# The last projection of a hybrid decoder layer in two sweeps, with seven products in place of eight in some of its quads

## The chip, the core and the metric

One core of a Trainium2 chip runs the whole layer. The metric is device time in microseconds: the median of several executions, here 1580.53 us for the kernel before (three runs, 1578.45 to 1582.09).

## What is computed

One layer of a conditioned decoder on 256 tokens of width 2048, all in float32: a modulated RMS norm, one wide projection, a gated recurrent branch and a sliding-window attention branch, their merge, and a gated feed-forward part. The change touches the end of it:

```python
gate, up = jnp.split(h2 @ w_ffn_in[l], 2, axis=-1)        # 256 x 5632 each
x = x + g2 * ((jax.nn.silu(gate) * up) @ w_ffn_out[l])    # 5632 x 2048
...
return rms_norm(x, final_g)
```

The projection of this document is the product with `w_ffn_out`: 256 tokens (two row blocks of 128, `t`), 5632 hidden channels (44 k blocks of 128, `kt`) and 2048 columns (four column blocks of 512, `n`).

## The kernel before

**Products in parts.** TensorE multiplies in the reduced float32 format (`fp32r`). To keep precision each operand is split in a high part (a cast) and a low part (the difference), and a product is three matmuls: high x high, high x low, low x high (`mm3`, L320). The weights come from memory as raw float32 in pieces of 128 x 1024 (512 KB). ScalarE (ACT) casts the high part (`do_hi`, L271 to L280; the profile shows it as line 277) and VectorE (DVE) subtracts for the low part (`do_lo`, L282 to L293, line 289). The activations are split once, after they are made.

**Items and buffers.** Every piece of weight is an item, a tuple in the list `items`: source, columns, a function that issues its matmuls, what comes after it, whether its parts are kept, and a weight for the planner. `step(i)` (L300) writes the program for item i in this order: stages of earlier results that are due (`run_posts`, one stage of each per step), the load of item i+5, the high part of item i+3, the low part of item i+2, fetches of other streams, and the matmuls of item i. Each engine executes its own instructions in the order in which they were written. There are five raw buffers, four for high parts and three for low parts (L43), so these steps run ahead of the matmuls by that much and no more. A planner's clock with assumed costs (L64, L198) decides only where side work is placed that has no fixed position; in the last projection all that is placed so is the fetch of the residual and of the final gain.

**The gate and up projections.** 11 pairs of slabs (L1110). After each pair `up_f_post` (L1096) multiplies, transposes on TensorE, and `parts_of` (L870) makes high and low parts of 4 k blocks, `fh` and `fl`, the stationary operands of the last projection. These 22 tiles stay in a pool of 25 equal buffers (`b4`).

**The last projection.** A first sweep over all 44 k blocks makes three column blocks (n = 0, 1, 2) for both row blocks, in six PSUM banks (`pf`): per two k blocks two items from `w_f2a` (columns 0 to 1023) and one from `w_f2b` (two k blocks of columns 1024 to 1535). `first_blocks` (L1178) then adds these blocks to the residual `x2`, squares them for the norm on ACT and multiplies with the final gain, while a second sweep makes the last column block from `w_f2c` (`pl`). There the last eight k blocks (`EARLY` = 36 on) are computed for row block 0 only; their weights are kept. `early_rows` (L1219) adds what row block 1 has by then. Its last eight k blocks come at the very end, in two halves of 256 columns (`late`, L1224), while row block 0 is finished (`finish_first`, L1205). `finish_last` (L1234) ends row block 1. An add is a pair of DVE instructions: multiply with the gate `bcs[5]` (tile `pa`), then add to `x2` (L1167, L1169).

```python
for k, (l, w) in enumerate(((ah, hi), (ah, lo), (al, hi))):
    for _, n, c0 in mine:
        ...
        nc.tensor.matmul(
            fin[t, n], lhsT=l[:, rows(t)], rhs=w[:, c0:c0 + 512], start=kt == 0 and k == 0,
```

Of the kernel before, what the change touches and what calls it, by code (L numbers as in the profile page):

```python
# [9 lines left out]
F32 = mybir.dt.float32  # L10
# [56 lines left out]
@with_exitstack  # L67
def hybrid_layer(
    ctx: ExitStack, tc, vecs, x_t, x_r, ada_k, ada_t, ada_g, w_in, bv_row, bm_row, bg_row, lru_w, w_lru, w_att, w_o,
    w_f1, w_f2a, w_f2b, w_f2c, fg_row, out,  # L70
):
    nc = tc.nc
    ctx.enter_context(tc.manual_schedule())
# [33 lines left out]
    def rows(t):  # L107
        return slice(t * P, (t + 1) * P)
# [149 lines left out]
                    break  # L258


    items = []
    live = {}
    at = {"load": 0, "hi": 0, "lo": 0}

    def do_load(i):
        src, cols = items[i][0], items[i][1]
        raw = wp.tile([P, CH], F32, tag="raw", name=f"raw{i}", bufs=AHEAD - 1)
        nc.sync.dma_start(raw[:, :cols], src)
        live[i] = [raw, None, None, load_time(cols)]

    def do_hi(i):  # L271
        cols, keep = items[i][1], items[i][4]
# [4 lines left out]
        nc.scalar.copy(hi[:, :cols], live[i][0][:, :cols])  # L277
        clock["act"] = max(clock["act"], live[i][3])
        charge(0, cols * T_ACT)
        live[i][1], live[i][3] = hi, clock["act"]  # L280

    def do_lo(i):  # L282
        cols, keep = items[i][1], items[i][4]
# [5 lines left out]
        nc.vector.tensor_tensor(lo[:, :cols], raw[:, :cols], f32(hi[:, :cols]), op=ALU.subtract)  # L289
# [3 lines left out]
        live[i][0] = None  # L293

    def upto(what, fn, n):
        while at[what] < min(n, len(items)):
# [1 line left out]
            at[what] += 1  # L298

    def step(i):  # L300
        _, cols, mm, post, _, weight = items[i]
# [8 lines left out]
        end = clock["pe"] + cols * T_PE * weight  # L310
        mm(hi, lo)
        run_sides(end)
        clock["pe"] = end
        if post is not None:
            posts.append(post())

    def in_rows_of(bank):
        return bank.rearrange("p j n -> p (j n)")
# [7 lines left out]
    def add_slab(slab, name, act, k0, k1, post, in_rows=False, before=None, late=0):  # L326

        banks = []

        def products(a, b):  # L330
            def go(hi, lo):
                if a == k0 + late and before is not None:
                    before()
                if a == k0:
                    banks.extend(wtile(f"{name}_{k0}_{i}") for i in range(2))
                parts = [(kt, f) for kt in range(a, b) for f in range(2 if in_rows else 4)]
                if b == k1:
# [12 lines left out]
            return go  # L350

        for a in range(k0, k1, 2):
            b = min(a + 2, k1)
            items.append((
                slab[:, a * 512:b * 512], (b - a) * 512, products(a, b), (lambda: post(banks)) if b == k1 else None,
                False, 1,
            ))


# [719 lines left out]
        posts.append(rest())  # L1079


    f_hi, f_lo, silu = {}, {}, {}


    def h2act(kt):
# [10 lines left out]
    def up_f_post(s):  # L1096
        def post(banks):
            sg = silu.pop(s)
            for t in range(2):
                nc.vector.tensor_tensor(sg[:, t, :], in_rows_of(banks[t]), sg[:, t, :], op=ALU.mult)  # L1100
            yield 1.4, 0
            yield 0, 0
            pts = turned(sg, f"ft{s}_")
            yield 0, 0
            fh, fl = b4(f"fh{s}", F32R), b4(f"fl{s}", F32R)
            yield from parts_of(pts, fh, fl)
            f_hi[s], f_lo[s] = fh, fl
        return post

    for s in range(11):  # L1110
# [7 lines left out]
    def last_first():  # L1118
        ada_ffn.finish(streams[-1].fetch)
        last = hp.tile([P, 4, D], F32, tag="h", name="last")  # L1120
        fin["x2"], fin["fg"] = last[:, 0:2, :], last[:, 2, :]
        fin["ss"] = const.tile([P, 2, 5], F32, name="ss3")
        for n in range(3):
            for t in range(2):
                pool, tag = ((ps_w, "w"), (ps_m, "m"))[n // 2]
                fin[t, n] = pool.tile([P, 512], F32, tag=tag, name=f"pf{t}{n}")

    def fetch_last():
        yield 0, 0
# [2 lines left out]
            yield 0, 0  # L1132
            nc.sync.dma_start(fin["x2"][:, t, :], x1d[rows(t), :])


    N_HOLD = 4
    EARLY = NH - 2 * N_HOLD

    def out_products(jobs, t2=(0, 1), hold=None, after=None):

        def go(hi, lo):
            if hold is not None:
                hold.extend((hi, lo, j) for j in jobs)
            if jobs[0][0] == 0 and jobs[0][1] == 0:
                last_first()
                sides.append(Side(fetch_last()))
            for t in t2:
                for kt in sorted({j[0] for j in jobs}):
                    ah, al = fact(kt)
                    mine = [j for j in jobs if j[0] == kt]  # L1150
                    for k, (l, w) in enumerate(((ah, hi), (ah, lo), (al, hi))):
                        for _, n, c0 in mine:
                            if (t, n) not in fin:
                                fin[t, n] = mtile(f"pl{t}")
                            nc.tensor.matmul(  # L1155
                                fin[t, n], lhsT=l[:, rows(t)], rhs=w[:, c0:c0 + 512], start=kt == 0 and k == 0,
                                stop=kt == (EARLY if (t, n) == (1, 3) else NH) - 1 and k == 2,
                            )
            if after is not None:
                after()  # L1160
        return go

    def add_block(t, ps, c0, cols, dst=None):

# [10 lines left out]
        yield  # L1175
        nc.scalar.activation(y, x2, AF.Square, accum_out=fin["ss"][:, t, n:n + 1])

    def first_blocks():  # L1178
        for n in range(3):
            for t in range(2):  # L1180
                g = residual(t, n)
                next(g)
                yield 1.2, 0
                next(g, None)
                yield 0, 0.7
        for t in range(2):
            x2 = fin["x2"][:, t, :3 * 512]
            nc.vector.tensor_tensor(x2, x2, fin["fg"][:, :3 * 512], op=ALU.mult)
            yield 1.7, 0

    for kt in range(0, NH, 2):
        for i in range(2):
            items.append((w_f2a[kt + i], CH, out_products([(kt + i, 0, 0), (kt + i, 1, 512)]), None, False, 1))
        items.append((
            w_f2b[kt // 2], CH, out_products([(kt, 2, 0), (kt + 1, 2, 512)]),
            first_blocks if kt == NH - 2 else None, False, 1,
        ))
    held = []

# [58 lines left out]
            elif i < 2:  # L1258
                nc.scalar.dma_start(out[rows(1), cs], x2[:, cs])

    for kt in range(0, NH, 2):
        late = kt >= EARLY
        items.append((
            w_f2c[kt // 2], CH,
            out_products(
                [(kt, 3, 0), (kt + 1, 3, 512)], (0,) if late else (0, 1), held if late else None,
                last_rows if kt == NH - 2 else None,
            ),
            early_rows if kt == EARLY - 2 else None, late, 0.5 if late else 1,
        ))  # L1270


# [95 lines left out]
    sides.extend((hmod, ada, ada_ffn))  # L1368
    for i in range(len(items)):
        step(i)  # L1370
    finish_first()
    finish_last()


def _layout(i):
# [8 lines left out]
        return w.reshape(NK, P, n, 512).transpose(2, 1, 0, 3).reshape(n, P, NK * 512)  # L1384

    def pairs(w):
        return w.reshape(NH // 2, 2, P, 512).transpose(0, 2, 1, 3).reshape(NH // 2, P, CH)

    ada_w, ada_b = f("ada_w")[0], f("ada_b")[0]
    vecs = np.concatenate(  # L1390
# [17 lines left out]
        "w_f2b": pairs(w2[:, CH:CH + 512]), "w_f2c": pairs(w2[:, CH + 512:]),  # L1408
        "fg_row": f("final_g"),
    }  # L1410
    return {k: np.ascontiguousarray(v) for k, v in made.items()}
# [19 lines left out]
```

## Time and profile before

| | |
|---|---|
| median of three runs | 1580.53 us |
| the profiled execution | 1578.05 us |
| its span, first to last instruction | 1576.3 us |
| granted TensorE clock, mean | 0.998 |
| memory traffic | 394.73 MB read, 4.20 MB written |

The profile comes from one execution. Its page gives busy times of the engines (PE is TensorE's matmul, PEld its weight load, DVE VectorE, ACT ScalarE, SP the queue that issues loads) and the chain that ended last. Groups of instructions are listed as line, engine, operation, output and inputs, with count, busy time, mean duration of one, and the idle time before them with what ended it. Matmuls overlap, so their durations add up to more than the time they take.

### The profile page before, as it was taken

The numbers are of one execution on the slowest core, as the hardware profiler recorded it, in microseconds if no ns is written. First come the engines' busy times: TensorE is split into PE (matmuls) and PEld (weight loads), VectorE is DVE, ScalarE is ACT, GpSimd is POOL, SyncE is SP. The second block draws the span as 40 slices with busy tenths as digits, with TensorE's granted clock in tenths as the row PEclk, the third lists the DMA queues.
The fourth block names the chain that finished last, engine by engine and source line by source line (L and its number), as shares of the span: only waits on it lengthen the run. The fifth ranks groups of instructions, "written<-read, shape, count | busy, mean of one in ns | idle before, by whom it ended". The sixth has DMA issues, their size and how long they took to land.

```text
span 1576.3 us, 21711 instructions
## 1 busy us (share of the span) xinstructions
PE 1559.2 (99%) x8151; PEld 1338.9 (85%) x8151; DVE 1123.1 (71%) x1427; ACT 760.2 (48%) x960; POOL 3.8 (0%) x9
## 2 busy tenths in 40 slices
PE   8999999999999999999999999999999999999997
PEld 7999999998877878888888887888888888888886
DVE  7889989899888888998558985454544555444465
ACT  4654444767855455443456444444444444333343
POOL 0000000000000000000000000000000000000000
PEclk9999999999999999999999999999999999999999
DMA  9999987665877898998768996666666666655553
GB/s 366 352 325 333 341 305 267 233 238 166 291 270 254 291 321 295 355 343 292 277 214 274 336 343 208 190 187 195 190 187 188 188 190 248 215 199 189 198 187 121
DMA packets 112908, 400.37 MB, mean 254 GB/s; under 512 B 12433, under 2 KB 12577, under 8 KB 112417
## 3 DMA queue, kind: packets, MB, share of 16 engines
q1 hardware_dynamic: 112514, 398.46, 74.0%
q8 instruction: 64, 1.05, 0.3%
q10 hardware_dynamic: 288, 0.52, 0.1%
q14 instruction: 42, 0.34, 0.1%
HBM read 394.73 MB, written 4.20 MB: 253 GB/s over the span
## 4 chain that ended last, share of the span: by engine, by line
PE 95%; DMA 3%; DVE 1%; ACT 0%; issue 0%; SPq 0%; DVEq 0%; ACTq 0%
PE pf L1155 11%; PE wi L324 6%; PE wi L323 6%; PE wi L322 6%; PE fu L322 5%; PE fu L323 5%; PE fu L324 5%; PE fg L324 5%; PE fg L322 5%; PE fg L323 5%; PE pl L1155 3%; PE wga L324 2%; PE wga L323 2%; PE wga L322 2%; PE wo L322 2%; PE wo L323 2%
## 5 line engine op out<-in xcount | busy, mean ns | idle before, releaser
L289 DVE TENSOR_TENSOR lo<-raw,hi 128x1024 fp32r<-128x1024 f32 (+1 forms) x540 | 650.1, 1207 | 390.3 <-PE pf L1155 95.6
L277 ACT CAST hi<-raw 128x1024 fp32r<-128x1024 f32 (+1 forms) x540 | 560.8, 1040 | 744.1 <-PE fu L324 141.8
L322 PE MATMUL wi<-h_both,hi 128*128 128x256 f32 x800 | 227.4, 284 | 1.7 <-ACT acc L498 1.7
L324 PE MATMUL wi<-h_both,lo 128*128 128x256 f32 x800 | 226.7, 283 | 2.0 <-DVE lo L289 2.0
L323 PE MATMUL wi<-h_both,hi 128*128 128x256 f32 x800 | 226.4, 283 | 0.0
L324 PEld LDWEIGHTS wi<-h_both,lo 128*128 128x128 f32 x800 | 153.5, 192 | 2.4 <-DVE lo L289 2.4
L322 PEld LDWEIGHTS wi<-h_both,hi 128*128 128x128 f32 x800 | 153.5, 192 | 2.1 <-ACT acc L498 1.9
L323 PEld LDWEIGHTS wi<-h_both,hi 128*128 128x128 f32 x800 | 153.5, 192 | 0.2
L322 PE MATMUL fg<-hi,h_both 128*128 128x512 f32 x352 | 138.4, 393 | 0.1
L322 PE MATMUL fu<-hi,h_both 128*128 128x512 f32 x352 | 137.8, 391 | 0.0
L324 PE MATMUL fg<-hi,h_both 128*128 128x512 f32 x352 | 137.1, 389 | 0.0
L323 PE MATMUL fg<-lo,h_both 128*128 128x512 f32 x352 | 137.0, 389 | 0.0
L324 PE MATMUL fu<-hi,h_both 128*128 128x512 f32 x352 | 137.0, 389 | 0.0
L323 PE MATMUL fu<-lo,h_both 128*128 128x512 f32 x352 | 136.9, 389 | 0.0
L409 DVE CUSTOM_DVE_ANT_0 aw<-aw,crow,modc 128x1024 f32<-128x1024 f32 x79 | 100.9, 1280 | 5.2 <-DMA aw<-in_ada_t_dram 5.2
L409 DVE CUSTOM_DVE_ANT_0 aw<-aw,crow,vec 128x1024 f32<-128x1024 f32 x79 | 100.6, 1278 | 3.6 <-DMA aw<-in_ada_t_dram 3.6
L1155 PE MATMUL pf<-hi,fh 128*128 128x512 f32 x264 | 88.5, 389 | 0.0
L1155 PE MATMUL pf<-hi,fl 128*128 128x512 f32 x264 | 88.4, 389 | 0.0
L1155 PE MATMUL pf<-lo,fh 128*128 128x512 f32 x264 | 88.4, 389 | 0.0
L322 PEld LDWEIGHTS fu<-hi,h_both 128*128 128x128 f32 x352 | 66.1, 188 | 14.1 <-issue 0.5
L323 PEld LDWEIGHTS fu<-lo,h_both 128*128 128x128 f32 x352 | 66.1, 188 | 14.1 <-issue 0.5
L324 PEld LDWEIGHTS fg<-hi,h_both 128*128 128x128 f32 x352 | 66.1, 188 | 14.0 <-DVE h_both L1054 0.2
(243 smaller groups left out, 2418.9 us busy)
## 6 DMA issues: line engine op xcount, KB each, us to landing
raw<-in_w_f_dram SPq DMA_DIRECT2D x176, 512.0 KB, 3.5
raw<-in_w_in_dram SPq DMA_DIRECT2D x164, 512.0 KB, 6.8
aw<-in_ada_t_dram SPq DMA_DIRECT2D x158, 512.0 KB, 6.3
raw<-in_w_f2a_dram SPq DMA_DIRECT2D x44, 512.0 KB, 3.2
raw<-in_w_lru_dram SPq DMA_DIRECT2D x32, 512.0 KB, 6.6
raw<-in_w_att_dram SPq DMA_DIRECT2D x32, 512.0 KB, 8.4
raw<-in_w_o_dram SPq DMA_DIRECT2D x32, 512.0 KB, 4.4
aw<-in_ada_g_dram SPq DMA_DIRECT2D x32, 512.0 KB, 6.6
```

The lines of the kernel that those rows point to most:

```text
L277: nc.scalar.copy(hi[:, :cols], live[i][0][:, :cols])
L289: nc.vector.tensor_tensor(lo[:, :cols], raw[:, :cols], f32(hi[:, :cols]), op=ALU.subtract)
L322: nc.tensor.matmul(ps, lhsT=lh, rhs=rh, start=start, stop=False, skip_group_check=True)
L323: nc.tensor.matmul(ps, lhsT=lh, rhs=rl, start=False, stop=False, skip_group_check=True)
L324: nc.tensor.matmul(ps, lhsT=ll, rhs=rh, start=False, stop=stop, skip_group_check=True)
L409: nc.vector.tensor_tensor_reduce(out=r, in0=r, in1=crow[:, j * CH:(j + 1) * CH], op0=ALU.mult, op1=ALU.add, scale=1.0, scalar=dst if j els ...
L1155: nc.tensor.matmul(fin[t, n], lhsT=l[:, rows(t)], rhs=w[:, c0:c0 + 512], start=kt == 0 and k == 0, stop=kt == (EARLY if (t, n) == (1, 3) e ...
```

## The change

The last projection goes in two sweeps of 1024 columns, n = 0 and 1 from `w_f2a`, then n = 2 and 3 from a new array `w_f2d` (the first 36 k blocks of columns 1024 to 2047). The last eight k blocks of n = 2 and n = 3 stay as they were, four items from `w_f2b` and four from `w_f2c`.

A quad is two row blocks x two k blocks x two column blocks: eight products of a 128 x 128 block with a 128 x 512 block, 24 matmuls. In 8 of the 22 quads of the first sweep and 8 of the 18 in the second (k = 6, 10, ..., 34, `SEVEN`) it is done by Strassen's scheme in Winograd's form with seven products, 21 matmuls. Its quad has four items in place of two: the two raw pieces (of the first only 512 columns are used by itself) and two pieces of differences that DVE makes from them. The seven stationary operands are the blocks and their sums (`fs`, made in `up_f_post` from the transposed activations), which are split into parts again in each sweep (`parts_high` on ACT, `parts_low` on DVE), two and one or two items ahead. Four products (p, q, r, u) accumulate over all eight quads in four PSUM banks of their own, the other three go to the blocks' own banks. After the last such quad of a sweep `combined` adds them up: a copy on ACT, four sums and four add pairs on DVE, in six stages. In the second sweep `early_rows` follows as a seventh.

The item tuple becomes a class. In `step` a new stage `made` stands between load and high part and writes the differences for item i+4, and the items' `before` functions stand behind the low part. The differences lie in the unused fourth row of the tile `last`. `first_blocks` becomes `blocks(n0, n1)`: residual, squares and gain for n = 0 and 1 after the first sweep, and for n = 2 after the last full item.

```diff
+N_MADE, N_HOLD = 5, 4
+SEVEN = tuple(range(6, 36, 4))
+EARLY = NH - 2 * N_HOLD
...
+    def do_made(i):
+        src = items[i].src
+        if callable(src):
+            clock["dve"] = max(clock["dve"], live[i - 1][3])
+            live[i][0] = src(i)
...
         upto("load", do_load, i + AHEAD)
+        upto("made", do_made, i + N_MADE)
         upto("hi", do_hi, i + N_HI)
         upto("lo", do_lo, i + N_LO)
+        for stage in it.before:
+            charge(*stage())
...
+            fc, fs = b4(f"fc{s}", F32R, (2, 2, S)), b4(f"fs{s}", F32, (8, P))
+            nc.scalar.copy(fc[:, 0], pts[0])
+            nc.scalar.copy(fs[:, 0:2, :], pts[1][:, :, 0:P])
+            nc.scalar.copy(fs[:, 2, :], pts[1][:, 1, P:])
+            yield 0, 1.3
+            nc.vector.tensor_tensor(fc[:, 1], pts[0], f32(fc[:, 0]), op=ALU.subtract)
...
+            nc.vector.tensor_tensor(s1, a21, a22, op=ALU.add)
+            nc.vector.tensor_tensor(s3, a21, a11, op=ALU.subtract)
+            nc.vector.tensor_tensor(s2, s1, a11, op=ALU.subtract)
+            nc.vector.tensor_tensor(s4, a12, s2, op=ALU.subtract)
...
+        def parts_high():
+            made["hi"] = wp.tile([P, 8, P], F32R, tag="araw", name=f"ah{sweep}_{k}", bufs=N_ADA)
+            nc.scalar.copy(made["hi"][:, 0:7, :], f_sum[k][:, 0:7, :])
+            return 0, 0.9
+
+        def parts_low():
+            made["lo"] = b4(f"al{sweep}_{k}", F32R, (8, P))
+            nc.vector.tensor_tensor(
+                made["lo"][:, 0:7, :], f_sum[k][:, 0:7, :], f32(made["hi"][:, 0:7, :]), op=ALU.subtract
+            )
+            return 1.0, 0
...
+        def first(i):
+            x = fin["made"][:, 0:CH]
+            a, b = live[i - 2][0], live[i - 1][0]
+            made["a"], made["b"] = a, b
+            nc.vector.tensor_tensor(x[:, 0:512], a[:, 512:], a[:, 0:512], op=ALU.subtract)
+            nc.vector.tensor_tensor(x[:, 512:], a[:, 512:], b[:, 512:], op=ALU.subtract)
...
+        def second(i):
+            y, x, b = fin["made"][:, CH:], made["x"], made["b"]
+            nc.vector.tensor_tensor(y[:, 0:512], b[:, 512:], x[:, 0:512], op=ALU.subtract)
+            nc.vector.tensor_tensor(y[:, 512:], b[:, 0:512], y[:, 0:512], op=ALU.subtract)
+            return y
+
+        items[-3].before.append(parts_high)
+        items[-2].before.append(parts_low)
+        half = 0.5
+        items.append(Item(src[k], CH, products((0, 0, "p")), weight=half / 2, used=512))
+        items.append(Item(src[k + 1], CH, products((1, 0, "00"), (6, 512, "01")), weight=half))
+        items.append(Item(first, CH, products((3, 0, "r"), (5, 512, "u")), weight=half))
+        items.append(Item(
+            second, CH, products((4, 0, "q"), (2, 512, "10")), (lambda: combined(n)) if k == SEVEN[-1] else None, weight=half,
+        ))
...
+        yield 0, 0.6
+        add(0, 0, pq)
+        nc.vector.tensor_tensor(pq, fin["q"], pq, op=ALU.add)
+        yield 1.8, 0
+        nc.vector.tensor_tensor(pqu, fin["u"], pq, op=ALU.add)
+        nc.vector.tensor_tensor(pqr, fin["r"], pq, op=ALU.add)
+        nc.vector.tensor_tensor(pqur, fin["r"], pqu, op=ALU.add)
+        yield 1.8, 0
+        add(0, 1, pqr)
+        yield 1.2, 0
+        add(1, 0, pqu)
+        yield 1.2, 0
+        add(1, 1, pqur)
...
+    for n, src in ((0, w_f2a), (2, w_f2d)):
+        for k in range(0, NH if n == 0 else EARLY, 2):
+            if k in SEVEN:
+                seven(k, n, src)
+                continue
+            for kt in (k, k + 1):
+                items.append(Item(
+                    src[kt], CH, out_products([(kt, n, 0), (kt, n + 1, 512)]), blocks(0, 2) if kt == NH - 1 else None,
+                ))
+    for i, k in enumerate(range(EARLY, NH, 2)):
+        items.append(Item(
+            w_f2b[i], CH, out_products([(k, 2, 0), (k + 1, 2, 512)]), blocks(2, 3) if k == NH - 2 else None,
         ))
```

More of the change, by code (lines that the diff above doesn't have):

```diff
@@ L282, in do_lo @@
     def do_lo(i):
-        cols, keep = items[i][1], items[i][4]
+        cols, keep = items[i].used, items[i].keep
         if keep:
@@ L309, in step @@
         clock["pe"] = max(clock["pe"], t)
-        end = clock["pe"] + cols * T_PE * weight
-        mm(hi, lo)
+        end = clock["pe"] + it.cols * T_PE * it.weight
+        it.mm(hi, lo)
         run_sides(end)
         clock["pe"] = end
-        if post is not None:
-            posts.append(post())
+        if it.post is not None:
+            posts.append(it.post())
     def in_rows_of(bank):
@@ L1120, in last_first, with bank @@
         last = hp.tile([P, 4, D], F32, tag="h", name="last")
-        fin["x2"], fin["fg"] = last[:, 0:2, :], last[:, 2, :]
+        fin["x2"], fin["fg"], fin["made"] = last[:, 0:2, :], last[:, 2, :], last[:, 3, :]
         fin["ss"] = const.tile([P, 2, 5], F32, name="ss3")
[L1123 to L1126, printed above, removed]
+    def bank(t, n):
+        if (t, n) not in fin:
+            fin[t, n] = (ps_w if n < 2 else ps_m).tile([P, 512], F32, tag="wm"[n // 2], name=f"pf{t}{n}")
+        return fin[t, n]
     def fetch_last():
@@ new lines, in combined, with add @@
+    def combined(n):
+        v = [b4(f"v{n}{i}", F32, (2, 512)) for i in range(2)]
+        pq, pqu, pqr, pqur = v[0][:, 0, :], v[0][:, 1, :], v[1][:, 0, :], v[1][:, 1, :]
+        nc.scalar.copy(pq, fin["p"])
+        def add(t, j, x):
+            y = sp.tile([P, 512], F32, tag="t2", name=f"yv{n}{t}{j}")
+            x2 = fin["x2"][:, t, (n + j) * 512:(n + j + 1) * 512]
+            nc.vector.tensor_tensor(y, x, bcs[5][:, (n + j) * 512:(n + j + 1) * 512], op=ALU.mult)
+            nc.vector.tensor_tensor(x2, y, x2, op=ALU.add)
+        yield 0, 0.6
[11 more added lines that the diff above has]
+        add(1, 1, pqur)
+        free(b4=2)
+        yield 1.2, 0
+        if n == 2:
+            yield from early_rows()
@@ L1259, in finish_last @@
                 nc.scalar.dma_start(out[rows(1), cs], x2[:, cs])
[L1261 to L1269, printed above, removed]
+    for i, k in enumerate(range(EARLY, NH, 2)):
+        items.append(Item(
+            w_f2c[i], CH,
+            out_products([(k, 3, 0), (k + 1, 3, 512)], (0,), held, last_rows if k == NH - 2 else None), keep=True, weight=0.5,
         ))
@@ L1370, in hybrid_layer @@
         step(i)
+    run_posts()
+    assert not posts
     finish_first()
```

101 lines of the change are left out of this document (63 added, 38 removed).

## The prediction, made before the result was known

> **What bounds the kernel now.** I read the page first, for the engine that is never free.
>
> ```profile
> span 1576.3 us, 21711 instructions
> ...
> PE 1559.2 (99%) x8151; PEld 1338.9 (85%) x8151; DVE 1123.1 (71%) x1427; ACT 760.2 (48%) x960; POOL 3.8 (0%) x9
> ...
> PE 95%; DMA 3%; DVE 1%; ACT 0%; issue 0%; SPq 0%; DVEq 0%; ACTq 0%
> ```
>
> PE is busy for 99% of the span and carries 95% of the chain that ended last. The change touches the last projection, so I looked at the chain from 1300 us on.
>
> ```profile
> 1327.27 5.44 PE pf L1155 x24
> 1332.71 0.87 PE ft L867 x8
> 1333.59 174.09 PE pf L1155 x768
> 1507.68 54.42 PE pl L1155 x240
> 1562.10 0.12 PE late L322
> ...
> 1567.87 0.02 issue
> 1567.89 0.44 DVE y L1167
> ...
> 1570.82 0.40 DVE last L1255
> ```
>
> The projection is 24 + 768 + 240 = 1032 matmuls of 512 columns without a gap, then 48 of 256 columns, then a short DVE and ACT tail. The pace is 174.09 / 768 = 0.2267 us for one matmul. (The groups of the page say 389 ns for one, but neighbours overlap: the pace is what a removed matmul gives back.)
>
> Next, what the other engines do there: the windows, the waits, and the queue that loads.
>
> ```profile
> 1333.59:1507.68 174.09, 174.09 (x769) 144.14 (x769) 79.85 (x68) 67.69 (x66) 0.00 (x0) 1.00 0.59 207
> 1507.68:1562.10 54.42, 54.42 (x243) 45.00 (x242) 35.03 (x34) 24.81 (x33) 0.00 (x0) 1.00 0.43 151
> ```
>
> ```profile
> ACT hi L277 <- PE pf L1155: 107.8, 65, 1.7
> DVE lo L289 <- PE pf L1155: 95.6, 64, 2.6
> ```
>
> ```profile
> SPq L268 <- DVE lo L289: 184.8, 81, 3.4
> ```
>
> The columns after a window's length are busy time of PE, PEld, DVE and ACT. In the first window DVE works 80 of 174 us and ACT 68. Both spend the rest waiting for PE to give back a buffer (95.6 us in 64 waits, 1.49 us each), and the loads in turn wait for DVE to free a raw buffer. So everything here is paced by PE, at a granted clock of 1.00, and a matmul that is not issued is time gained as long as DVE stays ahead. That is the question, because the change pays for the matmuls with DVE work.
>
> **PE: what is removed.** A quad of blocks (two row blocks of the tokens, two k blocks, two column blocks) had 8 products of 3 matmuls, 24 x 0.2267 = 5.44 us. With seven products it has 21, 4.76 us. In 16 quads 48 matmuls go: 48 x 0.2267 = 10.88 us. The eight-product quads only change order, and the loads keep their bytes and sizes (88 of 512 KB). The new products run three matmuls in a row on one bank, as the gate and up projections do already:
>
> ```profile
> L323 PE MATMUL fg<-lo,h_both 128*128 128x512 f32 x352 | 137.0, 389 | 0.0
> ...
> L1155 PE MATMUL pf<-hi,fh 128*128 128x512 f32 x264 | 88.5, 389 | 0.0
> ```
>
> One costs 389 ns in both orders, so I take the same pace. The Trainium skill (TensorE: Matmul & The Clock Gate, "Wait — 56ns, not 53.3ns?") gives 215.7 ns for 512 columns at the full clock; the trace paces them at 226.7, and by the page's figure, as an estimate, the cut would be 10.4 us.
>
> **DVE: what is added.** Its durations overlap as well, so I went to a stretch where it works without a break.
>
> ```profile
> 406.21 1.26 DVE L839 TENSOR_TENSOR gate<-wgl,bm 128x512 f32<-128x512 f32 x2
> 407.38 2.35 DVE L289 TENSOR_TENSOR lo<-raw,hi 128x1024 fp32r<-128x1024 f32 x2
> 409.65 1.22 DVE L713 TENSOR_TENSOR uc<-uc,acc 128x1024 f32<-128x1024 f32 x1
> ```
>
> ```profile
> 1556.68 0.69 DVE L1167 TENSOR_TENSOR y<-pl,pa 128x512 f32<-128x512 f32 x1 [4.83 <-PE pl L1155]
> 1557.41 0.69 DVE L1169 TENSOR_TENSOR last<-y,last 128x512 f32<-128x512 f32 x1
> 1558.02 2.35 DVE L289 TENSOR_TENSOR lo<-raw,hi 128x1024 fp32r<-128x1024 f32 x2
> ```
>
> From start to start a 1024-column subtraction takes (409.65 - 407.38) / 2 = 1.14 us. A 512-column one takes (407.38 - 406.21) / 2 = 0.585 to 1558.02 - 1557.41 = 0.61, so 0.60. One that reads what the instruction before it wrote starts 0.73 after that (1557.41 - 1556.68), so such a dependence costs 0.13 more. An 896-column one lies between, at 1.00 us.
>
> The seven-product quads alternate with eight-product ones. One such pair has six items in place of four, and this work for DVE: five low parts of 1024 columns (5.70), one of 512 for the first item (0.60), four 512-column differences of raw weights, one dependent (4 x 0.60 + 0.13 = 2.53), and the low part of the seven sums of activations (1.00). The sum is 9.83 us. PE has 45 matmuls in the pair, 10.20 us. So DVE goes from 4 x 1.14 of 10.88 us (42%) to 96%, with 0.37 us to spare per pair, some 34 ns for each of its 11 instructions. ACT:
>
> ```profile
> L277 ACT CAST hi<-raw 128x1024 fp32r<-128x1024 f32 x85 | 89.4, 1055 | 131.0 <-PE pf L1155 107.8 <-PE pl L1155 13.3 <-issue 6.3
> ...
> L873 ACT CAST fh<-ft 128x512 fp32r<-128x512 f32 x2 | 1.1, 586 | 0.0
> ```
>
> Five high parts at 1.055, one at 0.59 and the sums' high part at under 1.06 are 6.9 us of 10.20: no bound. Loads: four per 10.20 us, issued up to five buffers ahead, so this landing time stays covered.
>
> ```profile
> raw<-in_w_f2a_dram SPq DMA_DIRECT2D x41, 512.0 KB, 3.2
> ```
>
> The differences wait for two landed loads; behind them on DVE stand low parts that are needed two items later, and the loads left at least two items earlier. I price these waits at nothing; uncovered, each would cost up to 3.2 us less the 2.7 us of two short items.
>
> Does 96% hold under the buffers? There are three low-part buffers, so the low part of item i+3 starts when item i's matmuls have used theirs. The tightest case is the third item of a quad: behind it PE has 3 + 6 matmuls, 2.04 us, and one more before a low part is read (0.23), against 1.23 us for the subtraction. I walked the queue in program order with these times: each low part is ready 0.2 to 1 us before its matmul, so PE does not stop in the steady pairs. That is my forecast for them.
>
> **Where DVE falls behind.** Two places have more than the steady work.
>
> Start of the second sweep: the first sweep's two column blocks are added to the residual there, during the first three quads. DVE must do, up to the low part of the second item of the first seven-product quad, four add pairs (4 x 1.33), two 1024-column products with the final gain (2.28), both pairs of differences (2.53), the sums' low part (1.00) and six low parts (5 x 1.14 + 0.60): 17.4 us. PE needs 72 + 3 + 1 matmuls, 17.2 us. With a hand-over of about 0.2 us at the start the stall is 0.4 us.
>
> The end: the second sweep's seven products are combined while only four full items and four half items are left. Before the low part of the last half item DVE has six low parts (6.84), four add pairs and two residual pairs (6 x 1.33 = 7.98) and four combinations (2.53): 17.35 us, starting level. PE gets there after 48 + 18 + 1 matmuls, 15.2 us. So PE waits about 2.2 us at the last half item. Then a block of 1.33 and two products of 0.60 still stand in the queue, 2.5 us, against 1.4 us of matmuls. The residual of the first row block begins 1.2 us late, and these rows show what that meets:
>
> ```profile
> 1565.80 0.48 DVE L1216 TENSOR_SCALAR last<-last,r 128x512 f32<-128x512 f32 x1
> 1566.19 0.42 DVE L1167 TENSOR_TENSOR y<-late,pa 128x256 f32<-128x256 f32 x1
> 1566.64 0.42 DVE L1169 TENSOR_TENSOR last<-y,last 128x256 f32<-128x256 f32 x1
> 1567.89 0.42 DVE L1167 TENSOR_TENSOR y<-late,pa 128x256 f32<-128x256 f32 x1 [0.82 <-PE late L324]
> ```
>
> DVE had 0.82 us of slack before the last product; 1.2 late leaves 0.4 us on the end.
>
> Everything else I cost at nothing. The first sweep's combination (four pairs and four sums, 7.9 us) runs beside four quads of eight products, where DVE has 5.44 - 2.28 = 3.2 us free in each; uncovered it would cost the excess over 12.6 us, so nothing below that. The new preparation of eight slabs of activations replaces two subtractions by one and four of 128 columns, and runs beside the gate and up projections:
>
> ```profile
> 1000.00:1150.00 150.00, 150.00 (x676) 124.47 (x675) 74.62 (x68) 63.51 (x67) 0.00 (x0) 1.00 0.62 190
> ```
>
> DVE is half idle there. Even at 0.69 us for each of the four, a slab takes 2.1 us more; uncovered, the eight would cost 17 us, which a window with half of DVE free and PE busy throughout excludes.
>
> **The sum.** -10.88 + 0.4 + 2.2 + 0.4 = -7.9 us. The profiled execution took 1578.05 us (its span 1576.3 and 1.75 around it), so it would become 1570.2. It lies 2.5 us under the median of the runs, 1580.53; for the median I predict **1572.6 us**. A measurement of this kernel can tell about 0.2%, 3.2 us, from no change.
>
> **The rivals.**
>
> *DVE becomes the bound.* If instructions on DVE ran one after the other with their whole durations, a pair would need the sum of these:
>
> ```profile
> L289 DVE TENSOR_TENSOR lo<-raw,hi 128x1024 fp32r<-128x1024 f32 x86 | 105.1, 1225 | 108.8 <-PE pf L1155 95.6 <-PE pl L1155 11.3 <-issue 1.8
> L1169 DVE TENSOR_TENSOR last<-y,last 128x512 f32<-128x512 f32 x7 | 4.8, 692 | 0.2
> ```
>
> That is 5 x 1.225 + 5 x 0.692 + 1.09 = 10.68 us, 0.48 over PE's 10.20, in 16 pairs 7.7 us. The result is -0.2: no change, 1580.3. Against it stand the two back-to-back subtractions that took 2.27 us together, not 2.45; for it, that many of the new ones come with several waits, which that stretch shows less of. Chance 0.14. This is what the Trainium skill states (VectorE: DVE Perf Modes, "The DRAIN you can't avoid"): the next operation does not start until the pipe has emptied. It adds that an operation that is not held starts earlier, and the rows above show that case.
>
> *Slower: the hand-overs between DVE, ACT and PE.* In a seven-product quad a weight goes raw, difference (DVE), high part (ACT), low part (DVE), PE, and DVE's queue is in order. If one wait for PE of the present size, 1.49 us, survives per pair, with the next pair's differences and sums behind it, DVE needs 9.83 + 1.49 = 11.32 us; 16 x 1.12 = 17.9 us, so +10.0 and 1590.5. It turns the sign once such waits pass 0.37 + 7.9 / 16 = 0.86 us per pair. For it: three buffers now cover as little as 15 matmuls. Against it: DVE waits for PE today because it is early, and work moved ahead fills exactly that time. Chance 0.09.
>
> *No stall at the end or start.* If the combinations hide, the whole 10.9 us is gained: 1569.6. The queue order speaks against it. Chance 0.08.
>
> *The change doesn't do what it says:* 21 matmuls on freshly made parts take as long as 24 did. Then only the 3.0 us of stalls are left, 1583.5. The equal rows of 389 ns speak against it. Chance 0.04.
>
> **How the numbers follow.** The forecast keeps 0.65. Its own spread: stalls from 0 to 6 us (half of the first rival's 7.7 on top of 3), and 1.6 us on either side for where a median of runs falls (those shown reach from 1578.45 to 1582.09). The range goes from 1569.6 - 1.6 = 1568.0 to the first rival's 1580.3, rounded to 1580.5; it leaves out the two slower cases, 0.13, and a little at its ends. Faster by over 0.2%: 0.65 and 0.08, 0.73. Slower by over 0.2%: 0.09 and some of the 0.04, 0.12. The rest, 0.15, is the same within 0.2%.
>
> **What would show it.** In the profile after: 984 matmuls of 512 columns in this stage at 0.2267 us; DVE above nine tenths and PE without waits through both sweeps; waits of PE for a low part, about 0.4 us early in the second sweep and 2.2 us at the last half item; the DVE tail 0.4 us longer. I am wrong if PE waits for low parts in every pair (DVE's start-to-start times or hand-overs were too small), if the matmuls pace at over 0.2267, or if the last half item starts without a wait.

## The result, and the profile after

The kernel after took 1570.92 us (median of six runs, 1570.00 to 1574.08) and the kernel before 1580.30 us beside it (six runs, 1578.45 to 1582.09). The medians lie 9.4 us apart. The ratio of all runs is 0.9945, interval 0.9933 to 0.9958, which is 8.7 us less (6.6 to 10.6); that is the figure used below. The forecast was 1572.6 us, 7.9 us less, with a range of 1568.0 to 1580.5. The profiled execution of after took 1573.62 us, where 1570.2 was forecast.

From the page of after, the span, the engines and the shares of the chain that ended last:

```profile
span 1571.5 us, 21843 instructions
PE 1552.6 (99%) x8103; PEld 1332.7 (85%) x8103; DVE 1219.9 (78%) x1589; ACT 798.8 (51%) x1018; POOL 3.8 (0%) x9
PE 94%; DMA 3%; DVE 2%; ACT 0%; issue 0%; SPq 0%; DVEq 0%; ACTq 0%
```

48 matmuls are gone (8151 to 8103), DVE has 97 us more, and PE is the bound as before. The chain of after from 1300 us on:

```profile
1329.57 5.44 PE pf L1194 x24
...
1553.18 1.15 DVE lo L313
1554.38 1.57 PE pf L1194 x5
...
1563.10 0.43 DVE y L1293
...
1566.02 0.40 DVE last L1393
```

I measure the changed part as one stage: from the first matmul of the projection to the end of the last DVE instruction. Before it is 1570.82 + 0.40 - 1327.27 = 243.95 us; after it is 1566.42 - 1329.57 = 236.85 us, 7.10 less. The span fell by only 4.8 us, because this execution reached the projection 2.3 us later (1329.57 against 1327.27). Up to there the change touches only the preparation of the slabs, and that cost nothing: from the first product of the gate projection (`fg`) to the stage it is 492.8 us in both profiles (834.5 to 1327.27 before, 836.8 to 1329.57 after). The 2.3 us arose earlier, and the twelve profiles of after and its variants start the stage anywhere between 1326.0 and 1330.5 us. So the stage tells small differences that whole times don't.

Inside the chain stands something new: one low part of DVE, 1553.18. The waits of PE in the projection of after, and the windows (PE, PEld, DVE, ACT, POOL, granted clock, DMA share, GB/s) of a stretch in each sweep and of the end:

```profile
PE pf L1194 <- DVE lo L313: 2.0, 1, 2.0
```

```profile
1345.00:1425.00 80.00, 80.00 (x354) 66.24 (x353) 76.94 (x85) 51.42 (x56) 0.00 (x0) 1.00 0.61 205
1460.00:1540.00 80.00, 80.00 (x355) 66.24 (x354) 77.82 (x87) 52.83 (x57) 0.00 (x0) 1.00 0.59 201
1554.30:1555.90 1.60, 1.52 (x6) 1.25 (x7) 1.56 (x4) 0.00 (x0) 0.00 (x0) 0.88 0.00 0
1555.90:1559.00 3.10, 3.10 (x17) 3.10 (x16) 2.25 (x4) 0.72 (x2) 0.00 (x0) 0.51 0.00 0
```

PE is full in both sweeps and DVE at 76.94 / 80 = 96%, as forecast. PE waits once, 2.0 us, at the last half item. Then the granted clock falls to 0.51 for some 3 us, which was not forecast.

DVE's own timeline over one pair of quads (start, duration; in brackets the idle time before an instruction) shows what the 96% consist of:

```profile
1392.16 0.68 DVE L1238 TENSOR_TENSOR last<-raw 128x512 f32<-128x512 f32 x1
1392.77 0.69 DVE L1239 TENSOR_TENSOR last<-raw,raw 128x512 f32<-128x512 f32 x1
1393.37 0.68 DVE L313 TENSOR_TENSOR lo<-raw,hi 128x512 fp32r<-128x512 f32 x1
1393.97 1.08 DVE L1217 TENSOR_TENSOR al<-fs,ah 128x896 fp32r<-128x896 f32 x1
1394.97 0.68 DVE L1245 TENSOR_TENSOR last<-raw,last 128x512 f32<-128x512 f32 x1
...
1397.44 1.23 DVE L313 TENSOR_TENSOR lo<-last,hi 128x1024 fp32r<-128x1024 f32 x1
1398.95 1.23 DVE L313 TENSOR_TENSOR lo<-last,hi 128x1024 fp32r<-128x1024 f32 x1 [0.29 <-ACT hi L301]
...
1402.36 0.68 DVE L1238 TENSOR_TENSOR last<-raw 128x512 f32<-128x512 f32 x1
```

From one pair to the next it is 10.20 us, exactly PE's 45 matmuls (45 x 0.2267), and DVE's only pause is 0.29 us, a wait for ACT. From start to start the pause costs 1398.95 - 1397.44 - 1.14 = 0.37 us, so without it DVE needs 9.83 us for a pair. Where an instruction does not read what the one before it wrote, the start-to-start time is shorter than the duration (0.60 for 0.69, 1.00 for 1.08): whoever adds up durations finds DVE overfull here.

### The profile page after: what moved, and what is told of

Read it like the earlier page. It is cut to its first block, busy times and chain, and to the rows that moved or that the text cites. A ratio compares the mean times of both kernels' runs of the same rounds, so it can differ in the third digit from the quotient of the medians.

```text
span 1571.5 us, 21843 instructions
## 1 busy us (share of the span) xinstructions
PE 1552.6 (99%) x8103; PEld 1332.7 (85%) x8103; DVE 1219.9 (78%) x1589; ACT 798.8 (51%) x1018; POOL 3.8 (0%) x9
## 4 chain that ended last, share of the span: by engine, by line
PE 94%; DMA 3%; DVE 2%; ACT 0%; issue 0%; SPq 0%; DVEq 0%; ACTq 0%
PE pf L1194 9%; PE wi L350 6%; PE wi L348 6%; PE wi L349 6%; PE fu L348 5%; PE fu L350 5%; PE fu L349 5%; PE fg L348 5%; PE fg L350 5%; PE fg L349 5%; PE wga L350 2%; PE wga L349 2%; PE wo L348 2%; PE wga L348 2%; PE wo L349 2%; PE wa L349 2%
## 5 line engine op out<-in xcount | busy, mean ns | idle before, releaser
L301 ACT CAST hi<-raw 128x1024 fp32r<-128x1024 f32 (+1 forms) x540 | 554.0, 1027 | 646.0 <-PE fu L350 141.8
L313 DVE TENSOR_TENSOR lo<-raw,hi 128x1024 fp32r<-128x1024 f32 (+1 forms) x540 | 640.1, 1191 | 285.3 <-PE fu L349 91.1
L348 PEld LDWEIGHTS fu<-hi,h_both 128*128 128x128 f32 x352 | 66.1, 188 | 14.1 <-issue 0.5
L350 PEld LDWEIGHTS fg<-hi,h_both 128*128 128x128 f32 x352 | 66.1, 188 | 14.0 <-DVE h_both L1079 0.2
L350 PEld LDWEIGHTS fu<-hi,h_both 128*128 128x128 f32 x352 | 66.1, 188 | 13.8
L348 PEld LDWEIGHTS fg<-hi,h_both 128*128 128x128 f32 x352 | 66.1, 188 | 13.7 <-ACT h_both L1074 0.3
L349 PEld LDWEIGHTS fg<-lo,h_both 128*128 128x128 f32 x352 | 66.1, 188 | 13.5 <-issue 0.2
```

The costliest lines, as they stand in the source:

```text
L348: nc.tensor.matmul(ps, lhsT=lh, rhs=rh, start=start, stop=False, skip_group_check=True)
L349: nc.tensor.matmul(ps, lhsT=lh, rhs=rl, start=False, stop=False, skip_group_check=True)
L350: nc.tensor.matmul(ps, lhsT=ll, rhs=rh, start=False, stop=stop, skip_group_check=True)
```

## The experiments

Two theories stood at the start. **A**, that of the prediction: the gain is the 48 matmuls, DVE just keeps up in the pairs, and what is lost is lost at the end. **B**: DVE, or its hand-overs, bounds the pairs too, and the gain is cut there.

**The kernel after once more.**

> The changed kernel once more, as the yardstick for the three runs beside it. Both theories: 9 to 10 us under the kernel before (ratio 0.994 to 0.995), one wait of PE for a low part, 2.0 us, at the last half item, and a granted clock near 0.5 for some 3 us after it.

1571.79 us, ratio to before 0.9953 (0.9939 to 0.9966), stage 236.86 us; the end wait is 2.0 us and the clock falls again. By this ratio the gain is 7.4 us (5.4 to 9.6), less than the 9 to 10 expected. The gain is real and the stage repeats within 0.01 us.

**No seven-product quad.** The two sweeps stay, all quads have eight products.

```diff
-SEVEN = tuple(range(6, 36, 4))
+SEVEN = ()
```

`early_rows` then follows the last early item, and the stop of the last early bank moves along.

> The two sweeps of 1024 columns alone, all 40 quads with eight products, no differences and no sums. Theory A (the gain is the 48 matmuls, the new order is free): 1032 matmuls as in the kernel before, no wait of PE in the last projection, the time within 0.2% of the kernel before. Rival (part of the gain comes from the new order of sweeps and of the tail): 2 us or more under the kernel before.

1579.73 us, ratio 1.0004 (0.9996 to 1.0013). Its chain begins and ends the stage with these rows:

```profile
1329.95 5.44 PE pf L1194 x24
...
1573.47 0.40 DVE last L1393
```

The stage is 243.92 us, that of before (243.95), with no wait of PE. The new order of the sweeps is worth nothing by itself; the whole gain is the products.

**Fourteen quads.** The last seven-product quad of each sweep has eight products again, so combining starts four items earlier.

```diff
-SEVEN = tuple(range(6, 36, 4))
+SEVEN = tuple(range(6, 32, 4))
```

The stop of the last early bank moves along (`EARLY - 2` becomes `EARLY`).

> The last seven-product quad (k = 34) of each sweep goes back to eight products: 14 quads in place of 16, 6 matmuls more, 1.36 us. Theory A (PE sets the pace in the steady pairs; only the queue of DVE at the end of the second sweep costs, 2.0 us of wait and 1.5 us of slower clock behind it): DVE has one more quad with 3.2 us to spare before the end, the wait goes, and the time is 1.36 - 3.5 = 2.1 us below the changed kernel. Theory B (the wait is only where the load of DVE shows; it moves into the last rows): the wait goes but the end comes no earlier, +1.4 us. Theory C (DVE sets the pace in all pairs already): every pair that is given up frees DVE, more than 3 us below.

> The kernel with 14 seven-product quads once more, beside the next one. No wait of PE in the last projection; from its first matmul to the last instruction of DVE 234.4 us as before, and 0.9945 or a little less of the kernel before.

The first run gave 1570.74 us, 0.9956 (0.9943 to 0.9968), the second 1570.37 us, 0.9945 (0.9932 to 0.9957). In the chain:

```profile
1330.37 5.44 PE pf L1194 x24
...
1528.47 27.20 PE pf L1194 x120
...
1564.38 0.40 DVE last L1393
```

The stage is 234.41 us (234.40 in the second), 2.44 less than after with six matmuls more, and PE does not wait. It is also the price of a matmul: 243.95 - 14 x 3 x 0.2267 = 234.43 us, within 0.02 of the measured stage. By the same price sixteen quads without any stall would take 243.95 - 10.88 = 233.07 us, so after loses 3.78 us at its end. In whole times the versions can't be told apart.

**PE kept busy in the wait.** Nine more matmuls into a spare bank, ahead of the one that waits.

```diff
+if jobs[0][:2] == (NH - 2, 3) and kt == NH - 2 and k == 0:
+    fill = in_rows_of(wtile("fill"))
+    for _ in range(9):
+        nc.tensor.matmul(fill, lhsT=ah[:, rows(0)], rhs=hi[:, 0:512], start=True, stop=True)
```

> Nine matmuls into a spare PSUM bank, of which nothing is used, stand in front of the second matmul of the last half item, where PE waited 2.0 us. If that idle time is what lowers the granted clock, the 256-column matmuls at the end keep 0.12 us each and the time falls by 1.4 us against the changed kernel, with DVE's queue unchanged. If the clock falls for another reason, the time stays within 0.3 us.

1570.27 us, 0.9953 (0.9940 to 0.9965). The chain's first and last rows of the stage:

```profile
1326.89 5.44 PE pf L1194 x24
...
1561.84 0.40 DVE last L1397
```

That is 235.35 us, 1.50 less than after. The last matmuls of 256 columns (minimum, median and maximum duration), first in after, then here:

```profile
L348 PE MATMUL late<-hi,fh x16: 280/285/415, 1555.7 to 1562.5; 128*128 128x256 f32 x16
```

```profile
L348 PE MATMUL late<-hi,fh x16: 278/283/283, 1553.0 to 1558.3; 128*128 128x256 f32 x16
```

The 3.78 us of after are thus 1.50 of slower clock and 2.28 of the wait and what follows from it: in the timeline of PE of after the matmul before the wait starts at 1551.98 and the next at 1554.38, 2.17 later than the pace. The remaining 0.1 is put down to a later tail. That the nine matmuls kept the clock up is not shown by this one profile, because in three of the six profiles with an unfilled wait (table below) the clock stays up as well. The price of the fall doesn't hang on it: with the gain left out (below) the wait is there, the clock stays, and the stage is 235.35 us too.

**The subtraction of the sums' low part twice.** Does DVE really stand next to the bound?

```diff
+            for _ in range(2):
                 nc.vector.tensor_tensor(
                     made["lo"][:, 0:7, :], f_sum[k][:, 0:7, :], f32(made["hi"][:, 0:7, :]), op=ALU.subtract
                 )
```

> The low part of the seven sums is subtracted twice into the same place, 1.00 us of DVE more in each pair of quads. Theory A (DVE has 9.83 of 10.20 us, a slack of 0.37 per pair): PE waits for low parts in every pair, 0.6 us each, 9 to 10 us in 16 pairs, and the time comes back to the kernel before within 3 us. Rival (DVE has much more room, because its idle time in the trace is longer than the sum says): under 3 us more than the changed kernel. Rival (hand-overs between the engines already bind): 16 us more or above.

1583.27 us, 1.0025 (1.0016 to 1.0035): the gain is gone, and by more than expected: 3.9 us over before (2.5 to 5.5), where within 3 was expected. The stage is 246.69 us, 9.84 over after, and 11.3 over the 235.35 us that the same end wait leaves where the clock stays (gain left out, below). PE's waits, the window and DVE's timeline:

```profile
PE pf L349 <- DVE lo L313: 6.3, 15, 0.5
PE pf L1194 <- DVE lo L313: 2.1, 1, 2.1
```

```profile
1345.00:1425.00 80.00, 77.22 (x332) 61.58 (x331) 79.51 (x88) 48.66 (x52) 0.00 (x0) 1.00 0.57 191
```

```profile
1383.24 0.69 DVE L1239 TENSOR_TENSOR last<-raw 128x512 f32<-128x512 f32 x1
...
1385.05 2.21 DVE L1218 TENSOR_TENSOR al<-fs,ah 128x896 fp32r<-128x896 f32 x2
1387.18 0.68 DVE L1246 TENSOR_TENSOR last<-raw,last 128x512 f32<-128x512 f32 x1
...
1394.18 0.68 DVE L1239 TENSOR_TENSOR last<-raw 128x512 f32<-128x512 f32 x1
```

The pair now takes 10.94 us, 0.74 more (16 x 0.74 = 11.8), and DVE has no pause in it. PE waits 0.4 us in each of 15 pairs by the first row, which counts idle time alone; the longer pair shows the whole loss. The two subtractions take 1387.18 - 1385.05 = 2.13 us, the one in after 1.00, so 1.13 was added (the second writes where the first did). Without it DVE needs 10.94 - 1.13 = 9.81 us for a pair, where 9.83 was forecast: a second measurement of the slack, which does not use the sum.

**A small subtraction more**, 128 columns in each seven-product quad.

```diff
+            nc.vector.tensor_tensor(
+                made["lo"][:, 0, :], f_sum[k][:, 0, :], f32(made["hi"][:, 0, :]), op=ALU.subtract
+            )
```

> The changed kernel with one more DVE subtraction of 128 columns in each seven-product quad, about 0.2 us, so 10.0 of 10.20 us in a pair. Theory A (0.37 us of slack per pair): PE shows no new wait in the pairs and a pair still takes 10.20 us; only the wait at the last half item stays. Rival (DVE has no slack left, the pairs are level by chance): each pair gets 0.2 us longer, 3 us in all.

One execution: 1571.49 us, stage 236.93 us. The window, the added subtraction, and the first instruction of two pairs, one after the other:

```profile
1345.00:1425.00 80.00, 80.00 (x355) 66.24 (x354) 79.19 (x94) 51.94 (x56) 0.00 (x0) 1.00 0.64 207
```

```profile
1359.38 0.69 DVE L1241 TENSOR_TENSOR last<-raw 128x512 f32<-128x512 f32 x1
...
1362.31 0.29 DVE L1220 TENSOR_TENSOR al<-fs,ah 128x128 fp32r<-128x128 f32 x1
...
1369.58 0.69 DVE L1241 TENSOR_TENSOR last<-raw 128x512 f32<-128x512 f32 x1
```

DVE is at 79.19 of 80 us and the pair still takes 10.20. Some 0.3 us more per pair costs nothing, 1.13 costs 0.74: the bound lies between, where the forecast's slack of 0.37 has it. Theory B is out for after, and A's margin is as thin as it said.

**Less DVE work at the start of the second sweep.** If DVE carries a debt from there to the end, taking 2.28 us away there shortens the end wait. Once the two products with the final gain go to GpSimd, once they are left out (the first two column blocks of the output then lack the gain).

```diff
-                nc.vector.tensor_tensor(x2, x2, fin["fg"][:, n0 * 512:n1 * 512], op=ALU.mult)
+                eng = nc.gpsimd if n0 == 0 else nc.vector
+                eng.tensor_tensor(x2, x2, fin["fg"][:, n0 * 512:n1 * 512], op=ALU.mult)
```

```diff
+                if n0 > 0:
                     nc.vector.tensor_tensor(x2, x2, fin["fg"][:, n0 * 512:n1 * 512], op=ALU.mult)
```

> The two products of the first two column blocks with the final gain, 2.28 us of DVE at the start of the second sweep, go to GpSimd, which is idle there. Theory A in its sharper form (the second sweep as a whole has about 2 us more DVE work than PE work, wherever it stands): the lead of DVE carries over eight pairs to the end, the wait of 2.0 us shrinks to below 0.5 and the slower clock with it, 2.5 to 3.5 us below the changed kernel. Rival (only the work after the last seven-product quad counts, since DVE catches up in between): no change within 0.3 us. If GpSimd slows DVE while it works, DVE's instructions beside it get longer and PE waits early in the second sweep.

> The two products of the first two column blocks with the final gain are left out, 2.28 us of DVE at the start of the second sweep and nothing in their place. If a lead of DVE is carried through the pairs to the end, the wait at the last half item falls from 2.0 us to below 0.5. If DVE cannot run ahead by more than its three buffers, so that only the work after the last seven-product quad counts, the wait stays at 2.0 us.

On GpSimd: 1572.20 us, 0.9961 (0.9949 to 0.9974), stage 236.93 us. Left out: 1573.08 us in one execution, stage 235.35 us. The end wait stayed in both. On GpSimd, PE's waits and the rows of GpSimd (POOL) and DVE:

```profile
PE pf L1194 <- DVE lo L313: 2.0, 1, 2.0
PE pf L349 <- DVE lo L313: 1.3, 1, 1.3
```

```profile
1450.85 2.62 POOL L1320 TENSOR_TENSOR last<-last 128x1024 f32<-128x1024 f32 x1 [711.68 <-ACT y L1302]
1453.93 2.88 POOL L1320 TENSOR_TENSOR last<-last 128x1024 f32<-128x1024 f32 x1 [0.46 <-ACT y L1302]
```

```profile
1451.38 3.18 DVE L313 TENSOR_TENSOR lo<-raw,hi 128x1024 fp32r<-128x1024 f32 x1 [0.17 <-PE pf L1194]
1454.48 2.88 DVE L1238 TENSOR_TENSOR last<-raw 128x512 f32<-128x512 f32 x1
```

DVE lost (3.18 - 1.22) + (2.88 - 0.69) = 4.15 us beside GpSimd's two instructions to save 2.28, and a new wait of PE of 1.3 us came from it. That the stage is within 0.1 us of that of after is a coincidence: the clock did not fall here, and the new wait took its place. The Trainium skill (SBUF — State Buffer, "Who interferes with whom") names a reason: a DVE instruction with two inputs in SBUF gets the second one through a read interface shared with GpSimd. The stretched rows agree; both have two SBUF inputs.

Left out, nothing blocks DVE, and PE waits at the end as long as in after. PE's wait, and DVE in the first seven-product quad of the second sweep:

```profile
PE pf L1194 <- DVE lo L313: 2.0, 1, 2.0
```

```profile
1461.62 1.23 DVE L313 TENSOR_TENSOR lo<-last,hi 128x1024 fp32r<-128x1024 f32 x1 [1.28 <-PE pf L1194]
```

So no debt comes over from there, nor can a lead: with three low-part buffers DVE gets ahead by so much and then waits for PE, here 1.28 us, where it does not wait in after. The end wait is made by the work behind the last seven-product quad alone, which is what fourteen quads showed from the other side.

**The last six items' parts first.** All high and low parts that are left are written ahead of the combining work.

```diff
+        all_left = i >= len(items) - 6
-        upto("hi", do_hi, i + N_HI)
-        upto("lo", do_lo, i + N_LO)
+        upto("hi", do_hi, len(items) if all_left else i + N_HI)
+        upto("lo", do_lo, len(items) if all_left else i + N_LO)
```

> In the last six items the high and low parts of all that is left are written ahead of the adds, so that the last half item does not wait for DVE. Theory A: the wait of 2.0 us and the slow clock behind it go, but the adds stand later; from the first of the last eight items to the end DVE has some 24 us of work against 22 us of matmuls, so the last rows come 2 to 2.5 us later after the last matmul: 1 to 1.5 us under the changed kernel, and DVE, not PE, before the last rows in the chain. Rival (the adds hide under the last matmuls): 3.5 us under the changed kernel. Rival (all of it moves to the end): no change within 0.3 us.

1570.10 us, 0.9943 (0.9930 to 0.9957). The stage in the chain:

```profile
1326.62 5.44 PE pf L1195 x24
...
1561.58 0.40 DVE last L1394
```

That is 235.36 us, 1.49 less than after. PE does not wait and the clock does not fall, yet the stage stays 2.3 us above 233.07. DVE's rows:

```profile
1540.11 4.62 DVE L313 TENSOR_TENSOR lo<-raw,hi 128x1024 fp32r<-128x1024 f32 x4
...
1557.86 0.42 DVE L1294 TENSOR_TENSOR y<-late,pa 128x256 f32<-128x256 f32 x1
...
1558.66 0.42 DVE L1294 TENSOR_TENSOR y<-late,pa 128x256 f32<-128x256 f32 x1
```

PE's timeline has its last matmul at 1556.03, but the last product with the gate (the lower row) starts only at 1558.66, 2.6 us after it, behind DVE's queue, which waits 0.36 us for ACT in there (the norm of row block 0) and not for PE. The stall has moved from PE to the tail: what DVE has to do behind the last quad takes longer than PE's matmuls there, in either order. The three kernels with this DVE work and a steady clock (PE kept busy, gain left out, parts first) agree: 235.35, 235.35 and 235.36 us, wherever PE waits.

**And two DVE instructions fewer.** For n = 2 the combined sum is added to the residual once instead of twice.

```diff
-        add(0, 0, pq)
+        if n == 0:
+            add(0, 0, pq)
+        else:
+            fin["v", 0] = b4("v0p")[:, 0:2, :].rearrange("p a n -> p (a n)")
+            fin["v", 1] = pqu
+            nc.scalar.copy(fin["v", 0], fin["p"])
...
+        if n == 2:
+            v = fin["v", t]
+            nc.vector.tensor_tensor(v, ps, v, op=ALU.add)
+            ps = v
```

> 16 seven-product quads, the parts of the last six items ahead of the adds, and two DVE instructions less at the end: for the third column block the products' sum goes to the bank's sum first, and one add pair serves both. If DVE's total work after the last seven-product quad sets the end, two instructions of 0.60 us less bring the end 1.0 to 1.2 us forward against the same kernel without the merge: 234.2 to 234.4 us from the first matmul of the projection to the last instruction of DVE, level with 14 quads. If the late order alone sets it, 235.4 as without the merge.

1570.44 us, 0.9955 (0.9941 to 0.9969), stage 235.20 us: only 0.16 less than with the parts alone, a miss. DVE's timeline shows where most of it went:

```profile
1536.21 1.23 DVE L313 TENSOR_TENSOR lo<-raw,hi 128x1024 fp32r<-128x1024 f32 x1 [0.89 <-ACT hi L301]
```

ACT made one copy more than before, ahead of a high part, and DVE waited 0.89 us for that part. So this run does not settle whether DVE's total alone sets the end. Saved work on one engine became a wait for another.

The stages of all profiles together:

| kernel | stage, us | wait of PE at the end, us | clock falls there |
|---|---|---|---|
| before | 243.95 | none | no |
| after, and once more | 236.85, 236.86 | 2.0, 2.0 | yes, yes |
| no seven-product quad | 243.92 | none | no |
| fourteen quads, twice | 234.41, 234.40 | none | no |
| PE kept busy | 235.35 | filled | no |
| low part twice | 246.69 | 2.1 | no |
| small subtraction more | 236.93 | 2.0 | yes |
| gain on GpSimd | 236.93 | 2.0, and 1.3 earlier | no |
| gain left out | 235.35 | 2.0 | no |
| last parts first | 235.36 | none | no |
| and two instructions fewer | 235.20 | none | no |

## Why the prediction was right, step by step

**Forecast 7.9 us less; measured 8.7 (interval 6.6 to 10.6), and 7.10 in the profiled stages.** The whole-time interval holds both.

- *48 matmuls x 0.2267 = 10.88.* Right. The row of fourteen quads gives the price within 0.02 us for 42 matmuls, and the kernel without such quads shows that nothing else gains. The rival that fresh parts make matmuls as dear as 24 is out.
- *DVE 9.83 of 10.20 us per pair, no stop in the steady pairs.* Right: 9.81 worked out from the doubled subtraction, 96% busy, no wait of PE there. The timeline of after gives 9.83 as well, without its pause for ACT.
- *Rival "DVE becomes the bound", 10.68 per pair from whole durations.* Wrong by 0.87 us per pair, since instructions overlap in every quad, the new ones included. One further subtraction of 1.13 us would have made it true.
- *Rival of hand-overs.* One wait of 0.29 us for ACT's high part showed in the timeline of a pair (0.37 from start to start); it fits in the slack.
- *Rival "no stall at the end or start", 1569.6.* The median of 1570.92 alone does not exclude it. The trace does for the end, where PE waits 2.0 us; at the start it was right.
- *Preparation of the slabs at nothing.* Right: 492.8 us from the gate projection to the stage in both profiles.
- *0.4 us early in the second sweep.* Failed: no such wait. I let DVE begin the residual 0.2 us after the first sweep's end. DVE's timeline of after shows the first product earlier:

```profile
1443.15 0.69 DVE L1293 TENSOR_TENSOR y<-pf,pa 128x512 f32<-128x512 f32 x1 [0.30 <-PE pf L1194]
```

  The first sweep has 14 x 24 + 8 x 21 = 504 matmuls, 114.26 us, and 0.87 us of transposes lie in it as before, so it ends at 1329.57 + 115.13 = 1444.70. Row block 0's banks are done earlier than that, and DVE began 1.5 us before the sweep's end instead of 0.2 behind it, a difference of 1.7 us, more than the 0.4 of the forecast wait.
- *2.2 us at the last half item.* Right: 2.0 us of wait, 2.17 against the pace. Its cause, the queue behind the last such quad, is shown by fourteen quads (none) and by the parts written first (moved to the tail).
- *0.4 us of later tail.* Too large: about 0.1 with PE kept busy. The forecast let PE go on as soon as DVE was through with the low part; in after DVE's next instruction starts at 1554.24 and PE goes on at 1554.38, and these 0.14 us come off DVE's lateness. The rest of the difference was not followed up. In after it does not show, since the clock delays PE's last matmuls and DVE waits for them instead:

```profile
1563.10 0.42 DVE L1293 TENSOR_TENSOR y<-late,pa 128x256 f32<-128x256 f32 x1 [1.40 <-PE late L350]
```

- *Not in the sum:* the clock after the wait, 1.5 us.

Together -10.88 + 2.28 + 1.50 = -7.10. The forecast had 3.0 us of stalls. The end alone cost 2.28 where 2.2 + 0.4 was forecast, the start nothing, and the clock, which I had not seen, 1.50. So 0.7 us too much stands against 1.5 us missing, and part of the closeness of 7.9 is luck. With the stages in which the clock does not fall the sum is -8.6, and the forecast lies between the two.

## What to carry to other kernels

Before moving work from PE to DVE, add up DVE's work per recurring group by start-to-start times from a stretch where it is never idle, and hold it against PE's pace: here that told 96% from 105%, and gain from no change. Then look where the recurring group ends, because the combining work meets less and less matmul cover there and a lead can't be saved up beyond the buffers. Stop such a scheme some items before the end: fourteen quads gave a shorter stage than sixteen, though whole times don't tell the two apart.

## What the runs showed of the hardware

**A wait of 2 us can halve the clock.** In after, in its repeat and with the small subtraction, the granted clock fell after the end wait, to 0.51 over 3.1 us in the window above, and late matmuls went from 283 to 415 ns. In the seven profiles without an idle wait there it stayed up to the last matmul. With the gain on GpSimd, with the gain left out and with the doubled subtraction the wait is as long, 2.0 to 2.1 us, and the clock stays. A window shortly after the wait with the gain left out:

```profile
1555.00:1558.00 3.00, 2.69 (x17) 2.47 (x18) 2.96 (x6) 0.00 (x0) 0.00 (x0) 1.00 0.00 0
```

The Trainium skill (TensorE: Matmul & The Clock Gate, Part 1, the HAM clock gate) lets the clock fall after at least one idle window of about 3.4 us, and calls this window free-running. Three falls after 2.0 us of idle time speak against the length. That the clock falls after some waits and not after others of the same length would fit a window with a phase of its own, but what decides it was not tried.

**A GpSimd product of 128 x 1024 in float32 took 2.62 to 2.88 us** beside DVE's work (rows of GpSimd are rough), where DVE's start-to-start time is 1.14. The two-input subtractions of DVE that met them ended 1.09 us after GpSimd's first instruction and 0.55 us after its second (1454.56 - 1453.47, 1457.36 - 1456.81), close to what they take undisturbed, 1.14 and 0.60. So it looks as if each got going only when GpSimd was done.
